# A two-layer hybrid encoder in fp32: all sums of Strassen-like units by accumulating transfers, and two more units in the second mixer

## The chip, the core and the metric

The kernel runs on one core of a Trainium2 chip. The core has five engines that run beside one another, each with its own in-order queue: TensorE (PE; matmuls, with weight loads shown as PEld), VectorE (DVE), ScalarE (ACT), GpSimd (POOL) and SyncE (SP, which only issues transfers here). Transfers (DMAs) are issued by SP, POOL and ACT and run beside the engines; one that adds to its destination, called an accumulating transfer below, is issued by POOL in this kernel. The metric is the device time of one execution in microseconds (us), as the median of several runs.

## What is computed

Two layers over x of 256 positions by 2048 channels, in fp32. Layer 0 mixes with grouped-query attention, layer 1 with dilated windowed attention in three groups of eight heads; each is followed by a gated MLP of width 5632 with a width-3 convolution between its two projections.

```python
def mixer_b(h, w_qkv, w_o, rel_bias):
    qkv = (h @ w_qkv).reshape(b, s, n_g, 3, hg, HEAD_DIM)
    for g, (window, dil) in enumerate(B_GROUPS):
        o, lz = dilated_group(qkv[:, :, g, 0], qkv[:, :, g, 1], qkv[:, :, g, 2], ...)
    ...
    return y @ w_o

def conv_ffn(h, w_up, conv_w, conv_b, w_down):
    u = conv(h @ w_up) + conv_b
    gate, val = jnp.split(u, 2, axis=-1)
    return (jax.nn.silu(gate) * val) @ w_down

for i in range(DEPTH):
    hn = rms_norm(h, mix_norm[i])
    h = h + (mixer_a(hn, ...) if i % 2 == 0 else mixer_b(hn, ...))
    h = h + conv_ffn(rms_norm(h, ffn_norm[i]), ...)
return rms_norm(h, final_norm)
```

## The kernel before

**Matmuls.** All weights stream from DRAM once. A piece of 128 x 1024 fp32 numbers (512 KB) is loaded by SP into a `raw` buffer (a ring of four), and split into a high half `wh` on ACT and a low half `wl` = raw - wh on DVE (rings of four each). Each fp32 product is then three matmuls: high by high, high by low, low by high. `feed` (L142) does this for one group of 512 input channels (`kg`) and 512 output columns: two pieces, 24 matmuls of 128 x 512 in the order in which the pieces come. The splits are given a higher priority, so they stand on ACT and DVE some pieces ahead of their matmuls; how far is limited by the rings.

**Units.** For two column blocks that share their input, one `kg` can be done as a unit: a seven-product scheme on the 2 x 2 blocks b11, b12, b21, b22 of the weights and sums of the inputs. The products, numbered 1, 2, 3, 5, 7, 6, 4 in the order of the code, take 6 matmuls each, 42 in all, where the two plain feeds take 48. Four of the weights that they multiply are sums: t1 = b11 + b12 (product 5), b12 + b22 (product 7), t6 (product 6) and t4 (product 4). `fast_unit` (L190) loads the four blocks and makes the sums with four DVE adds (L204). `home_unit` (L219) makes most of them by transfers: SP loads b11 into t1 and b12 into the second half of a `home` tile, POOL issues accumulating transfers onto b12 (L246) and, after product 1, onto t1 (L248). With two `own` tiles, `middle` (called after the unit's first feed) issues t6 += b12 on POOL (L251) and loads b21 into the other tile by SP (L252), and `rest` does products 2 to 4, with one DVE add (L239) for t4.

**Pairs.** `up_pair` (L636) does a pair of column blocks with a unit for `kg` 0 and plain feeds for `kg` 1 to 3, in an order given by a table: `UP_ORDER` has three feeds of one side, the unit, and three feeds of the other. It then makes the two blocks of the unit's results with folds. The MLP uses it for the gate and value blocks of eight of its eleven pairs of blocks per layer (`UP`), with `home` and `own` tiles; its up and down projections run in two halves (pairs 0 to 5, then 6 to 10), so pair 6 is the first behind the first half's down projection, and its `own` tiles take buffers that the down projection has read. The second mixer (`mixer_b`) runs in two halves (`hf`) of four heads for each of three groups (`g`); `MIX` lists the (hf, g) whose key and query blocks are done as a pair with `fast_unit`, after (0, 0), for which the sums of the inputs are made. (1, 0) makes these sums again and is done plainly, and so are the three value blocks of each half.

**What sets the order.** A scheduler puts each engine's instructions into a fixed order; generators in `pending` and `beside` are advanced one step between feeds, and so place the attention work among the matmuls. On a queue an instruction that waits holds up those behind it. POOL issues the accumulating transfers, and also copies transposed blocks (`tT`, `kT`, `qT`: keys and queries; `wide`: for the values; `u` in the MLP), turns a one-hot table into matmul form in the first MLP (L1368, CAST `oh`, read by PE at L1377), and adds down-projection partial sums to a DRAM copy of the residual (`away`, L325). The residual `h` is kept in the buffers `h0` and `h1`, which are put away in DRAM during some stages (`put_away`, `fetch`) and serve as homes then.

Of the kernel before, what the change touches and what calls it, by code (L numbers as in the profile page):

```python
# [14 lines left out]
P = 128  # L15
# [11 lines left out]
MIX = (0, 1), (0, 2), (1, 1), (1, 2)  # L27
# [9 lines left out]
def tile_encoder(ctx: ExitStack, tc: tile.TileContext, x, xT, w_a, w_ao, q_gain, k_gain, w_b, w_bo,  # L37
# [104 lines left out]
    def feed(accs, lhs, kg, wap, first, last, by_m=False, pieces=1, mid=None, begun=()):  # L142
        raws, w = [], 2048 // pieces
# [10 lines left out]
        def mms(order):  # L154
            for m, kt in order:
                (wh, wl), j = hls[kt // 2], kt % 2
                xh, xl = lhs[4 * kg + kt][:2]
                st, sp = first and kt == 0 and m not in begun, last and kt == 3
# [60 lines left out]
    def home_unit(acc, pick, wap0, wap1, begun, home, end=(1,), own=None):  # L219
# [24 lines left out]
        if own:  # L244
            nc.sync.dma_start(flat(own[0]), wap0[:, :1024])
# [4 lines left out]
        def middle():  # L250
            nc.gpsimd.dma_start(flat(own[0]), flat(b12), accum_op=ALU.add)  # L251
            nc.sync.dma_start(flat(own[1]), wap0[:, 1024:])  # L252

        def rest(end, steps=False):
            if own:
                (t6, b21), b22 = own, raw_tile()
            else:
                b21, b22 = raw_tile(), raw_tile()
                t6 = b22
                nc.sync.dma_start(flat(b21), wap0[:, 1024:])  # L260
            nc.sync.dma_start(flat(b22), wap1[:, 1024:])
            for i, (q, r) in enumerate(((2, b21), (3, b22), (5, t1), (7, b12), (6, t6), (4, b21))):
# [3 lines left out]
                elif q == 7:  # L266
                    total(b21, t6, b21)
# [3 lines left out]
        return (middle, rest) if own else rest  # L271
# [351 lines left out]
    def sums_made(lhs, kg, at, st, picks):  # L623
        own = [pair_slot(at + 2 * i, [P, 4, 2, P], F32R, "s") for i in range(2)]
# [11 lines left out]
    def up_pair(w, ns, lhs, order, picks, junk, fold_tile, first_done, home=None, own=None):  # L636
# [5 lines left out]
        sides = (a2, a4), (a3, a8)  # L642
        tt = nc.vector.tensor_tensor
        for i, (kg, side) in enumerate(order):
            later = {s for _, s in order[i + 1:]}
            if side is None:
# [3 lines left out]
                if home is not None:  # L650
                    rest(end)
                else:
                    fast_unit(acc, picks[kg], w[ns[0], kg], w[ns[1], kg], begun, end, None)
            else:
                mine = ((2, 4), (3, 8))[side]
                feed(sides[side], lhs, kg, w[ns[side], kg], not begun.issuperset(mine),
                     not later & {side, None}, begun=[m for m in range(2) if mine[m] in begun])
                begun.update(mine)
                if i == 0 and home is not None:
                    middle()  # L660
# [18 lines left out]
    def ffn(l, hT, ss_in, cw, g_next, last, side=None):  # L679
        with tc.tile_pool(name=nm("fpool"), bufs=1) as fp:  # L680
# [181 lines left out]
            for hf, (p0, p1) in enumerate(HALVES):  # L862
# [41 lines left out]
                def post(n):  # L904
# [8 lines left out]
                    elif hf == 1:  # L913
                        sumsq_cols(ss, n, junk)
                        start(late_transpose(hTn, n, g_next, fp, "cg", lambda: quad_tile(fp, "quad", 2)))

# [465 lines left out]
    def mixer_b(hT, ss_in):  # L1382
        with tc.tile_pool(name="bpool", bufs=1) as bp:
# [36 lines left out]

            cw, turn = load_taps(1)
            allp = slice(None)
            for hf in range(2):
# [167 lines left out]
                for g in range(3):  # L1591
                    bts = biases(hf, g)
                    ns = 6 * g + 2 + hf, 6 * g + hf
                    if (hf, g) in MIX:
# [8 lines left out]
                        extra[0] = ((hpool, ["a0", "a1"]), (hpool, ["a6", "a7"]), (bp, ["e0", "e1"]))[hf * g]  # L1603
                        qa = up_pair(w_b, ns, hT, MIX_ORDER if (hf, g) == (1, 1) else UP_ORDER, picks, junk, fold_tile, k_done)
                        extra[0] = None
# [118 lines left out]
```

## Time and profile before

| | |
|---|---|
| median of 3 runs | 2214.55 us (2213.77 to 2215.14) |
| profiled execution | 2213.77 us, of which the span is 2211.9 us |
| granted PE clock, mean | 0.999 of full speed |
| DVE, split wl<-raw,wh (L172) | 621 of 1236 ns |
| ACT, split wh<-raw (L171) | 621 of 1044 ns |

The span is the time from the first to the last instruction in the profile. Times in the prediction are those of the profiled execution, counted from the span's start. In the rows, a line such as `L252 SPq DMA_DIRECT2D own<-in_w_up_dram` names the source line, the engine (with q: its queue), the operation and output<-input by the program's names without buffer numbers; "us to landing" is the time from a transfer's issue until its data has arrived. A bracket at a row's end is the time for which the engine was idle before it, and what it then waited for.

### The profile page before, as it was taken

Reading aid. Unit: us, or ns where it says so; the run is one execution under the profiler, and the core shown is the slowest. Engines: PE = TensorE matmul, PEld = TensorE weight load, DVE = VectorE, ACT = ScalarE, POOL = GpSimd, SP = SyncE. Lnnn points to the kernel's source line nnn. Section 1 sums busy time; section 2 is a strip of 40 time slices with the busy share of each in tenths; the row PEclk is TensorE's granted clock in tenths of the full one; section 3 lists DMA queues with packets and bytes.
Section 4 is the critical chain, followed back from the end, with each engine's and each line's share of the span. In section 5 each row is a group of like instructions: output and inputs, shape, how many; then the busy total and the mean of one; then the engine's idle time right before and its main releaser. Section 6 shows DMA issues by size and latency. Waiting matters only on the chain.

```text
span 2211.9 us, 29227 instructions
## 1 busy us (share of the span) xinstructions
PE 2197.0 (99%) x9885; PEld 1821.6 (82%) x9885; DVE 1852.0 (84%) x2335; ACT 1549.9 (70%) x2360; POOL 634.9 (29%) x873
## 2 busy tenths in 40 slices
PE   9999999999999999999999999999999999999998
PEld 7888888888888888888888888888888888888877
DVE  6887779999778998978876878588899987799987
ACT  7667768787457887677756775567878865678764
POOL 3343324432103331041354216003333300223311
PEclk9999999999999999999999999999999999999999
DMA  8666868867988856665566555578777778977754
GB/s 303 194 214 214 274 211 256 246 201 220 284 249 267 238 197 220 209 200 195 184 202 198 173 181 186 193 237 260 229 253 223 224 228 256 299 206 246 232 193 143
DMA packets 141030, 494.13 MB, mean 223 GB/s; under 512 B 15944, under 2 KB 19784, under 8 KB 139856
## 3 DMA queue, kind: packets, MB, share of 16 engines
q1 hardware_dynamic: 125360, 437.44, 58.5%
q0 software_dynamic: 15232, 54.54, 12.0%
q8 instruction: 77, 1.26, 0.2%
q14 instruction: 73, 0.60, 0.1%
q10 hardware_dynamic: 288, 0.30, 0.0%
HBM read 470.09 MB, written 13.73 MB: 219 GB/s over the span
## 4 chain that ended last, share of the span: by engine, by line
PE 55%; DVE 3%; issue 1%; ACT 1%; DMA 0%; POOL 0%; POOLq 0%; DVEq 0%; ACTq 0%
PE acc L161 15%; PE acc L162 15%; PE acc L160 15%; DVE wl L172 1%; PE ps L234 1%; PE ps L233 1%; PE ps L232 1%; PE ps L213 1%; PE ps L212 1%; PE ps L214 1%; PE acc L234 1%; PE acc L233 1%; PE acc L232 1%; PE acc L213 1%; PE acc L214 1%
## 5 line engine op out<-in xcount | busy, mean ns | idle before, releaser
L172 DVE TENSOR_TENSOR wl<-raw,wh 128x1024 fp32r<-128x1024 f32 (+1 forms) x621 | 760.7, 1236 | 163.8 <-ACT wh L171 158.9
L171 ACT ACTIVATE wh<-raw 128x1024 fp32r<-128x1024 f32 (+1 forms) x621 | 642.1, 1044 | 255.3 <-PE acc L162 178.3
L160 PE MATMUL acc<-wh,xh 128*128 128x512 f32 x1668 | 651.5, 391 | 0.5 <-ACT wh L171 0.5
L161 PE MATMUL acc<-wl,xh 128*128 128x512 f32 x1668 | 651.2, 390 | 0.8 <-DVE wl L172 0.7
L162 PE MATMUL acc<-wh,xh 128*128 128x512 f32 x1668 | 650.0, 390 | 0.0
L161 PEld LDWEIGHTS acc<-wl,xh 128*128 128x128 f32 x1668 | 313.5, 188 | 67.3 <-DVE wl L172 3.9
L160 PEld LDWEIGHTS acc<-wh,xh 128*128 128x128 f32 x1668 | 313.6, 188 | 64.7 <-ACT wh L171 1.0
L162 PEld LDWEIGHTS acc<-wh,xh 128*128 128x128 f32 x1668 | 313.3, 188 | 64.5
L751 POOL COPY u<-quad 32x256 f32<-32x256 f32 x352 | 261.9, 744 | 237.5 <-DVE quad L491 219.4
L161 PE MATMUL acc<-wl,a 128*128 128x512 f32 x720 | 280.7, 390 | 1.1 <-DVE wl L172 1.1
L160 PE MATMUL acc<-wh,a 128*128 128x512 f32 x720 | 281.2, 391 | 0.0
L162 PE MATMUL acc<-wh,a 128*128 128x512 f32 x720 | 280.4, 390 | 0.0
L751 ACT ACTIVATE u<-quad 32x256 f32<-32x256 f32 x352 | 147.8, 420 | 20.5 <-DVE quad L491 15.7
L161 PEld LDWEIGHTS acc<-wl,a 128*128 128x128 f32 x720 | 135.3, 188 | 28.9 <-DVE wl L172 1.5
L162 PEld LDWEIGHTS acc<-wh,a 128*128 128x128 f32 x720 | 135.2, 188 | 28.3 <-DVE a L442 0.2
L160 PEld LDWEIGHTS acc<-wh,a 128*128 128x128 f32 x720 | 135.3, 188 | 27.4
L510 POOL COPY wide<-quad 32x256 f32<-32x256 f32 x88 | 53.2, 605 | 210.1 <-DVE quad L491 152.9
L226 ACT ACTIVATE wh<-home 128x1024 fp32r<-128x1024 f32 x65 | 68.2, 1056 | 51.6 <-PE acc L162 45.1
L495 POOL COPY wide<-quad 32x256 f32<-32x256 f32 x133 | 90.6, 681 | 41.6 <-DVE quad L491 31.5
L603 ACT ACTIVATE stg<-acc,rstd 128x512 f32<-128x512 f32 x122 | 80.1, 678 | 31.5 <-DVE acc L675 15.8
L227 DVE TENSOR_TENSOR wl<-home,wh 128x1024 fp32r<-128x1024 f32 x65 | 80.7, 1246 | 16.3 <-ACT wh L226 16.3
L739 DVE SCALAR_TENSOR_TENSOR cg<-u,cw,cg 128x256 f32<-128x256 f32 x176 | 81.7, 509 | 4.5 <-ACT cg L731 4.4
(418 smaller groups left out, 3446.5 us busy)
## 6 DMA issues: line engine op xcount, KB each, us to landing
raw<-in_w_up_dram SPq DMA_DIRECT2D x304, 512.0 KB, 5.2
raw<-in_w_down_dram SPq DMA_DIRECT2D x160, 512.0 KB, 5.4
raw<-in_w_b_dram SPq DMA_DIRECT2D x144, 512.0 KB, 4.7
raw<-in_w_bo_dram SPq DMA_DIRECT2D x48, 512.0 KB, 4.5
raw<-in_w_a_dram SPq DMA_DIRECT2D x40, 512.0 KB, 4.7
raw<-in_w_ao_dram SPq DMA_DIRECT2D x32, 512.0 KB, 4.8
own<-in_w_up_dram SPq DMA_DIRECT2D x32, 512.0 KB, 6.6
home<-in_w_up_dram SPq DMA_DIRECT2D x32, 512.0 KB, 5.1
```

Source lines behind the costliest of these rows:

```text
L160: nc.tensor.matmul(accs[m], xh, wh[:, j, :], start=st, stop=False)
L161: nc.tensor.matmul(accs[m], xh, wl[:, j, :], start=False, stop=False)
L162: nc.tensor.matmul(accs[m], xl, wh[:, j, :], start=False, stop=sp)
L171: nc.scalar.activation(wh[:, c], r[:, c], AF.Copy)
L172: newest[0] = nc.vector.tensor_tensor(wl[:, c], r[:, c], wh[:, c].bitcast(F32), ALU.subtract)
L226: nc.scalar.activation(wh, r, AF.Copy)
L227: newest[0] = nc.vector.tensor_tensor(wl, r, wh.bitcast(F32), ALU.subtract)
L495: nc.gpsimd.tensor_copy(o[32 * c:32 * c + 32, :, 32 * q:32 * q + 32], quad[32 * q:32 * q + 32, c])
L510: nc.gpsimd.tensor_copy(dst, src)
L603: evac[0] = nc.scalar.activation(o[:, m, :], accs[m], AF.Copy, scale=rstd[:, m:m + 1])
L739: nc.vector.scalar_tensor_tensor(cj, halves(flat[:, j, o:o + NT])[:, ::-1], tap(n, j, i), cj, ALU.mult, ALU.add)
L751: put(u[32 * c:32 * c + 32, :, :, 32 * q:32 * q + 32], quad[32 * q:32 * q + 32, c].rearrange("p (j m) t -> p j m t", m=2))
```

## The change

Four things are done.

1. In `home_unit` with `own` tiles, b21 is loaded into t4's tile at the unit's start; product 2 moves from the rest to right behind the first feed; t6 += b12 is issued there, and t4 += t6 is a POOL transfer issued after the next feed. The DVE add of t4 goes.
2. The second mixer's pairs use `home_unit` with `home` tiles in `h0` and `own` tiles in buffers that are free at that time, in place of `fast_unit` and its four DVE adds.
3. There are two more units in the second mixer: the keys and queries of (1, 0), done by `MIX_ORDER`, and the values of groups 0 and 1 of the first half, blocks 4 and 10.
4. For that, the residual goes to DRAM at the end of the first MLP and is fetched in the second half's value part. The sums of the inputs are made once, into `h1`, for both halves.

`feed`'s `last` becomes a list of blocks for which the accumulation ends.

```diff
@@ -24,7 +24,7 @@
 NRAW, NHL = 4, 4
 AHEAD = 60
 UP = 1, 2, 3, 4, 6, 7, 8, 9
-MIX = (0, 1), (0, 2), (1, 1), (1, 2)
+MIX = (0, 1), (0, 2), (1, 0), (1, 1), (1, 2)
 MIX_ORDER = (1, 0), (2, 0), (3, 0), (1, 1), (2, 1), (0, None), (3, 1)
 EVEN = range(0, 16, 2)
 UP_ORDER = (1, 0), (2, 0), (3, 0), (0, None), (1, 1), (2, 1), (3, 1)
@@ -140,6 +140,7 @@
         return x[m] if isinstance(x, tuple) else x[:, m * P:(m + 1) * P]
 
     def feed(accs, lhs, kg, wap, first, last, by_m=False, pieces=1, mid=None, begun=()):
+        last = last if isinstance(last, list) else [0, 1] if last else []
         raws, w = [], 2048 // pieces
         for i in range(max(pieces, 2)):
             if pieces < 4 or i % 2 == 0:
@@ -155,7 +156,7 @@
             for m, kt in order:
                 (wh, wl), j = hls[kt // 2], kt % 2
                 xh, xl = lhs[4 * kg + kt][:2]
-                st, sp = first and kt == 0 and m not in begun, last and kt == 3
+                st, sp = first and kt == 0 and m not in begun, m in last and kt == 3
                 xh, xl = of_m(xh, m), of_m(xl, m)
                 nc.tensor.matmul(accs[m], xh, wh[:, j, :], start=st, stop=False)
                 nc.tensor.matmul(accs[m], xh, wl[:, j, :], start=False, stop=False)
@@ -242,33 +243,41 @@
         nc.sync.dma_start(flat(t1), wap0[:, :1024])
         nc.sync.dma_start(flat(b12), wap1[:, :1024])
         if own:
-            nc.sync.dma_start(flat(own[0]), wap0[:, :1024])
+            t6, t4 = own
+            nc.sync.dma_start(flat(t6), wap0[:, :1024])
+            nc.sync.dma_start(flat(t4), wap0[:, 1024:])
         nc.gpsimd.dma_start(flat(b12), wap1[:, 1024:], accum_op=ALU.add)
         product(1, t1, end)
         nc.gpsimd.dma_start(flat(t1), wap1[:, :1024], accum_op=ALU.add)
 
-        def middle():
-            nc.gpsimd.dma_start(flat(own[0]), flat(b12), accum_op=ALU.add)
-            nc.sync.dma_start(flat(own[1]), wap0[:, 1024:])
+        def plain_steps():
+            product(2, t4)
+            nc.gpsimd.dma_start(flat(t6), flat(b12), accum_op=ALU.add)
+            yield
+            nc.gpsimd.dma_start(flat(t4), flat(t6), accum_op=ALU.add)
+            yield
+            yield
 
         def rest(end, steps=False):
             if own:
-                (t6, b21), b22 = own, raw_tile()
+                b21, b22, s6 = t4, raw_tile(), t6
+                seq = (3, b22), (5, t1), (7, b12), (6, s6), (4, b21)
             else:
                 b21, b22 = raw_tile(), raw_tile()
-                t6 = b22
+                s6 = b22
+                seq = (2, b21), (3, b22), (5, t1), (7, b12), (6, s6), (4, b21)
                 nc.sync.dma_start(flat(b21), wap0[:, 1024:])
             nc.sync.dma_start(flat(b22), wap1[:, 1024:])
-            for i, (q, r) in enumerate(((2, b21), (3, b22), (5, t1), (7, b12), (6, t6), (4, b21))):
+            for i, (q, r) in enumerate(seq):
                 product(q, r, end)
                 if q == 3 and not own:
                     total(b22, t1, b22)
-                elif q == 7:
-                    total(b21, t6, b21)
+                elif q == 7 and not own:
+                    total(b21, s6, b21)
                 if steps:
                     step(i % 2 == 0)
 
-        return (middle, rest) if own else rest
+        return (plain_steps(), rest) if own else rest
 
     def fold(acc, n0, n1, one, two):
         def hs(m, n):
@@ -621,7 +630,11 @@
         yield
 
     def sums_made(lhs, kg, at, st, picks):
-        own = [pair_slot(at + 2 * i, [P, 4, 2, P], F32R, "s") for i in range(2)]
+        if at is None:
+            t = hpool.tile([P, 2, 4, 2, P], F32R, tag="h1", name=nm("s"))
+            own = [t[:, i] for i in range(2)]
+        else:
+            own = [pair_slot(at + 2 * i, [P, 4, 2, P], F32R, "s") for i in range(2)]
         split_in_order(*own, st.rearrange("p i (j t) -> p i j t", j=2))
         pick = {q: tuple(tuple(lhs[4 * kg + b + j][i][:, m * P:(m + 1) * P] for j in range(2)) for i in range(2))
                 for q, b, m in ((1, 0, 0), (2, 2, 0), (4, 2, 1))}
@@ -633,13 +646,15 @@
         yield from sums_begun(lhs, kg, r, st)
         sums_made(lhs, kg, at, st, picks)
 
-    def up_pair(w, ns, lhs, order, picks, junk, fold_tile, first_done, home=None, own=None):
+    def up_pair(w, ns, lhs, order, picks, junk, fold_tile, first_done, home=None, own=None,
+                steps=False):
         (a2, a4), (a3, a8) = new_acc(), new_acc()
         acc, begun = {2: a2, 3: a3, 4: a4, 8: a8}, set()
         if home is not None:
             acc[1] = ps_tile()
             middle, rest = home_unit(acc, picks[0], w[ns[0], 0], w[ns[1], 0], begun, home, own=own)
         sides = (a2, a4), (a3, a8)
+        ended = [] if home is None else [2]
         tt = nc.vector.tensor_tensor
         for i, (kg, side) in enumerate(order):
             later = {s for _, s in order[i + 1:]}
@@ -648,16 +663,17 @@
                 end = [q for q, s in ((1, None), (5, None), (6, None), (7, None), (2, 0), (4, 0), (3, 1))
                        if not later & {None, s}]
                 if home is not None:
-                    rest(end)
+                    rest(end, steps)
                 else:
                     fast_unit(acc, picks[kg], w[ns[0], kg], w[ns[1], kg], begun, end, None)
             else:
                 mine = ((2, 4), (3, 8))[side]
                 feed(sides[side], lhs, kg, w[ns[side], kg], not begun.issuperset(mine),
-                     not later & {side, None}, begun=[m for m in range(2) if mine[m] in begun])
+                     [m for m in range(2) if not later & {side, *([None] if mine[m] not in ended else [])}],
+                     begun=[m for m in range(2) if mine[m] in begun])
                 begun.update(mine)
-                if i == 0 and home is not None:
-                    middle()
+                if home is not None and None in later:
+                    next(middle, None)
             if 0 in begun or not begun >= {1, 2} or later & {0, None}:
                 continue
             begun.add(0)
@@ -913,6 +929,8 @@
                     elif hf == 1:
                         sumsq_cols(ss, n, junk)
                         start(late_transpose(hTn, n, g_next, fp, "cg", lambda: quad_tile(fp, "quad", 2)))
+                        if n % 2:
+                            put_away(n // 2)
 
                 def done(accs, n):
                     add_residual(accs, n)
@@ -1417,6 +1435,10 @@
 
             def fold_tile():
                 return bp.tile([P, 2, 512], F32, tag="vh", name=nm("fold"))
+
+            def homes(pool, *tags):
+                return (hpool.tile([P, 4, 512], F32, tag="h0", name=nm("home")),
+                        [pool.tile([P, 2, 512], F32, tag=t, name=nm("own")) for t in tags])
 
             cw, turn = load_taps(1)
             allp = slice(None)
@@ -1600,25 +1622,35 @@
                             next(gen)
                             beside.append(gen)
 
-                        extra[0] = ((hpool, ["a0", "a1"]), (hpool, ["a6", "a7"]), (bp, ["e0", "e1"]))[hf * g]
-                        qa = up_pair(w_b, ns, hT, MIX_ORDER if (hf, g) == (1, 1) else UP_ORDER, picks, junk, fold_tile, k_done)
-                        extra[0] = None
+                        qa = up_pair(w_b, ns, hT, MIX_ORDER if hf and g < 2 else UP_ORDER, picks, junk, fold_tile, k_done,
+                                     *homes(*((hpool, "a0", "a1"), (hpool, "a2", "a3"), (hpool, "a6", "a7"),
+                                              (bp, "e0", "e1"))[hf * (g + 1)]))
                         start(s_gen(g, qa, kTs[0], bts))
                         continue
                     ka = project(w_b, ns[0], hT, kgs)
                     kT = pair_tile(bp, [P, 4, NT], "kT", 1, g > 0)
                     start(k_gen(ka, kT))
-                    if g == 0:
-                        beside.append(sums(hT, 0, 20, tmp(), tmp(), picks))
+                    beside.append(sums(hT, 0, None, tmp(), tmp(), picks))
                     start(s_gen(g, project(w_b, ns[1], hT, kgs), kT, bts))
                 if hf == 0:
                     start(turn)
-                v12 = [bp.tile([P, 2, 512], F32, tag=f"e{n}", name=nm("v12")) for n in range(2)]
-                for g in range(3):
-                    accs = project(w_b, 6 * g + 4 + hf, hT, kgs)
-                    vs[g] = evac_split(bp, accs, rstd, v12[g - 1] if g else None)
-                    if g == 0:
-                        start(value_stage())
+                def v_whole(g):
+                    return bp.tile([P, 2, 512], F32, tag=f"e{g - 1}", name=nm("v12"))
+
+                def v_done(accs):
+                    vs[0] = evac_split(bp, accs, rstd, None)
+                    start(value_stage())
+
+                if hf == 0:
+                    accs = up_pair(w_b, (4, 10), hT, MIX_ORDER, picks, junk, partial(v_whole, 2), v_done,
+                                   *homes(hpool, "a0", "a1"), True)
+                    vs[1] = evac_split(bp, accs, rstd, v_whole(1))
+                else:
+                    for i in range(2):
+                        fetch(i)
+                    v_done(project(w_b, 5, hT, kgs))
+                    vs[1] = evac_split(bp, project(w_b, 11, hT, kgs), rstd, v_whole(1))
+                vs[2] = evac_split(bp, project(w_b, 16 + hf, hT, kgs), rstd, v_whole(2))
 
             def own(kg):
                 return pair_tile(bp, [P, 4, NT], "qT" if kg else "kT")
```

`order` rows below list an engine's instructions as they stand in its queue: source line, operation, output<-input with buffer numbers, shape, and how many alike follow one another.

ACT, at the first pair of the second half of the first MLP (pair 6). `home_6003` is the unit's home, `own_6005` the tile of b21 and t4, `raw_...` are pieces of the feeds, `ps_6010` is the first product's accumulator. Before:

```order
L226 ACTIVATE wh_6015<-home_6003 128x1024
L171 ACTIVATE wh_6030<-raw_6026 128x1024
L171 ACTIVATE wh_6046<-raw_6028 128x1024
L171 ACTIVATE wh_6068<-raw_6064 128x1024
L171 ACTIVATE wh_6084<-raw_6066 128x1024
L666 ACTIVATE junk_6202<-ps_6010 128x512
L171 ACTIVATE wh_6104<-raw_6100 128x1024
L171 ACTIVATE wh_6120<-raw_6102 128x1024
L226 ACTIVATE wh_6141<-own_6005 128x1024
L226 ACTIVATE wh_6151<-raw_6139 128x1024
L226 ACTIVATE wh_6161<-home_6003 128x1024
```

After:

```order
L227 ACTIVATE wh_6016<-home_6003 128x1024
L172 ACTIVATE wh_6031<-raw_6027 128x1024
L172 ACTIVATE wh_6047<-raw_6029 128x1024
L682 ACTIVATE junk_6202<-ps_6010 128x512
L227 ACTIVATE wh_6063<-own_6005 128x1024
L172 ACTIVATE wh_6078<-raw_6074 128x1024
L172 ACTIVATE wh_6094<-raw_6076 128x1024
L172 ACTIVATE wh_6115<-raw_6111 128x1024
L172 ACTIVATE wh_6131<-raw_6113 128x1024
L227 ACTIVATE wh_6152<-raw_6150 128x1024
L227 ACTIVATE wh_6162<-home_6003 128x1024
```

The first split of `own_6005` stands behind the first feed's two pieces now, where it stood behind three feeds' six; the second and third feeds' splits stand behind it.

POOL, in the first MLP's third pair (pair 3): `home_3799` is its home, `own_3800` its t6, `own_3801` its t4, `oc_3690` the loaded one-hot table and `oh_3691` its matmul form. Before:

```order
L1363 DMA oc_3690<-in_onehot_dram 128x1024
L246 DMA home_3799<-in_w_up_dram 128x1024
L1368 CAST oh_3691<-oc_3690 128x1024
L251 DMA own_3800<-home_3799 128x1024
L751 COPY u_2642<-quad_3640 32x8x32 x8
L248 DMA home_3799<-in_w_up_dram 128x1024
```

After:

```order
L249 DMA home_3799<-in_w_up_dram 128x1024
L1381 DMA oc_3690<-in_onehot_dram 128x1024
L255 DMA own_3800<-home_3799 128x1024
L1386 CAST oh_3691<-oc_3690 128x1024
L767 COPY u_2642<-quad_3640 32x8x32 x8
L251 DMA home_3799<-in_w_up_dram 128x1024
L257 DMA own_3801<-own_3800 128x1024
```

The table's load and its CAST have each gone behind one of the unit's transfers: the CAST stands behind t6 += b12 (L255 after, L251 before), and t4 += t6 (L257) is new.

POOL, in the second half of the second mixer, where the first group's keys (`tT`, first of the two) and queries (second) are copied into place; `bt` are bias tables, `scr` is their place in DRAM. Before:

```order
L1405 DMA bt_2021_10753<-scr 128x2x128 x4
L1405 DMA bt_2022_10754<-scr 128x2x128 x4
L510 COPY tT_10980<-quad_10981 32x8x32 x8
L510 COPY tT_11166<-quad_11167 32x8x32 x8
L510 COPY kT_11491<-quad_11511 32x8x32 x8
```

After, with `home_11177`, `own_11178` and `own_11179` the home, t6 and t4 of the next pair, (1, 1):

```order
L1423 DMA bt_2022_10690<-scr 128x2x128 x4
L249 DMA home_11177<-in_w_b_dram 128x1024
L255 DMA own_11178<-home_11177 128x1024
L251 DMA home_11177<-in_w_b_dram 128x1024
L1423 DMA bt_2023_10691<-scr 128x2x128 x4
L519 COPY tT_11121<-quad_11122 32x8x32 x8
L257 DMA own_11179<-own_11178 128x1024
L519 COPY tT_11225<-quad_11226 32x8x32 x8
```

Three of the next pair's transfers and four bias loads stand ahead of the key copies, and t4 += t6 between the key and the query copies. L255 waits for the landing of L249, and L249 for that of SP's load into the same home.

## The prediction

> **What bounds the kernel now.** I read the page first: the busy shares and the chain that ended last, then what TensorE (PE) waits for.
>
> ```profile
> span 2211.9 us, 29227 instructions
> PE 2197.0 (99%) x9885; PEld 1821.6 (82%) x9885; DVE 1852.0 (84%) x2335; ACT 1549.9 (70%) x2360; POOL 634.9 (29%) x873
> ...
> PE 55%; DVE 3%; issue 1%; ACT 1%; DMA 0%; POOL 0%; POOLq 0%; DVEq 0%; ACTq 0%
> ...
> PE acc L161 <- DVE wl L172: 3.3, 6, 1.1
> ...
> PE ps L457 <- DVE qTl L442: 1.3, 2, 0.8
> ```
>
> PE is occupied for 99% of the span, and its largest waits come to a few us: 3.3 us in six waits for a weight's low half, 1.3 us in two waits for the low half of the queries. VectorE (DVE) is busy 84%, but since PE hardly waits for it, time taken off DVE alone is worth almost nothing. The time is the number of matmuls times their pace, and whatever makes PE wait is added in full, since PE has no slack in which to catch up. The pace stands in the timeline of PE, here where the second half of the first MLP begins:
>
> ```profile
> 640.32 0.39 PE L232 MATMUL ps<-wh,xh 128*128 128x512 f32 x1
> 640.55 0.39 PE L233 MATMUL ps<-wl,xh 128*128 128x512 f32 x1
> 640.78 0.39 PE L234 MATMUL ps<-wh,xh 128*128 128x512 f32 x1
> ...
> 647.12 0.39 PE L160 MATMUL acc<-wh,xh 128*128 128x512 f32 x1
> ```
>
> The listed 0.39 us is a pipelined length; from start to start it is 30 matmuls in 6.80 us, 0.227 us each.
>
> **What the change takes away.** Each unit does with 42 matmuls what two plain feeds do with 48. Two units more are 12 matmuls fewer: 12 x 0.227 = **-2.7 us**. On DVE 32 adds go:
>
> ```profile
> L239 DVE TENSOR_TENSOR own<-own,own x16: 1211/1224/1307, 312.9 to 2023.7; 128x1024 f32<-128x1024 f32 x16
> L204 DVE TENSOR_TENSOR raw<-raw,raw x22: 1210/1220/1305, 895.9 to 2152.4; 128x1024 f32<-128x1024 f32 x22
> ```
>
> All 16 of L239 and 16 of the L204 adds (those of the four mixer units) go, 32 x 1.22 = 39 us of DVE. On PE that is worth no more than the waits above: 3.3 + 1.3 = 4.6 us in all, most at places that the change does not touch. I take **-0.5 us** (0 to -2.5). The new issues on POOL and SP and six more splits on DVE go beside PE work, except where an in-order queue holds something that PE wants soon. These places are the rest of the sum.
>
> **First pair of the second half of each MLP (the largest term).** b21 is now wanted as product 2 right after the first feed. Its buffer is the one that the down projection's last feed has just read, so SP issues the load only when PE is done with that feed, in both kernels at the same place in SP's order. What it took, first MLP and second:
>
> ```profile
> L252 SPq DMA_DIRECT2D own<-in_w_up_dram x1: 328/328/328, 640.5 to 640.5; - x1
> ...
> DMA to landing us min/median/max: 9.0/9.0/9.0
> ...
> L252 SPq DMA_DIRECT2D own<-in_w_up_dram x1: 327/327/327, 1884.0 to 1884.0; - x1
> ...
> DMA to landing us min/median/max: 8.9/8.9/8.9
> ```
>
> Issued at 640.5, landed at 649.5. ACT and PE used it long after that:
>
> ```profile
> 650.04 1.06 ACT L226 ACTIVATE wh<-own 128x1024 fp32r<-128x1024 f32 x1 [1.66 <-PE acc L162]
> ...
> 658.00 0.39 PE L232 MATMUL acc<-wh,xh 128*128 128x512 f32 x1
> ```
>
> Now product 2 stands after 6 matmuls of product 1 and 24 of the first feed, so at 640.32 + 30 x 0.227 = 647.1. Landing 649.5, wh on ACT 1.06 more, 650.6; wl on DVE 1.22 more, 651.8. PE waits 3.5 us for wh, and its second matmul, which wants wl and is due at 647.4, waits about 1.0 us longer: **4.4 us**. In ACT's order the splits of the following feeds stand behind this one, so nothing is done ahead meanwhile. The same numbers hold at 1884.0. Two layers: **+8.8 us**. With the 6.6 us that is the median of all such loads, it would be 647.1 + 2.3 - 647.4 = 2.0 us each; the two rows of this place are nearer, and I keep 2.0 to 4.9 each.
>
> The Trainium skill ("DMA: Bandwidth & Descriptors", section "Anatomy of one DMA — SWDGE (gpsimd) path") gives a fit of 2.0 us plus the bytes over 436 GB/s; as an estimate by that page 512 KB would land 3.2 us after issue, and neither place would stall at all. The trace disagrees: 9.0 and 8.9 us here. The fit is for one DMA by itself; the sum does not use it.
>
> **The sum for product 4, same two places.** t4 += t6 is a transfer on POOL's queue, behind t6 += b12 and two accumulations of down-projection partial sums:
>
> ```profile
> L251 POOL DMA_DIRECT2D own<-home x1: 861/861/861, 647.5 to 647.5; - x1
> ...
> DMA to landing us min/median/max: 8.8/8.8/8.8
> ...
> L325 POOL DMA_DIRECT2D away<-fold x2: 1441/1702/1963, 648.0 to 648.6; - x2
> ...
> DMA to landing us min/median/max: 12.9/14.5/16.0
> ...
> 664.80 0.39 PE L232 MATMUL acc<-wh,xh 128*128 128x512 f32 x1
> ```
>
> t6 has landed at 647.5 + 8.8 = 656.3; only then is t4 += issued. It lands at 664.4 with the 8.0 of the group, or at about 669 with the 12.9 of its neighbours. Product 4 was due at 664.8, now 4.4 later, at 669.2, and needs the data 2.3 before, at 666.9. That is from -2.5 to +2.5; nearer to its own group's row, so **+0.6 us** each, **+1.2** together (0 to 2.5 each).
>
> **One-hot CAST in the first MLP (third pair).** On POOL the CAST now stands behind t6 += b12, which waits for the landing of b12's accumulation:
>
> ```profile
> 370.33 0.87 POOL L246 DMA_DIRECT2D home<-in_w_up_dram  x1 [2.81 <-DMA home<-in_w_up_dram]
> 373.33 1.15 POOL L1368 CAST oh<-oc 128x1024 fp32r<-128x1024 f32 x1 [2.12 <-DMA oc<-in_onehot_dram]
> 379.24 0.87 POOL L251 DMA_DIRECT2D own<-home  x1 [4.76 <-DMA home<-in_w_up_dram]
> ...
> 380.03 0.40 PE L1377 MATMUL ps<-oh,rh 128*24 128x512 f32 x1
> ```
>
> It moves from 373.3 to 379.24 + 0.87 = 380.1 and ends at 381.3; PE reads oh in its order at 380.03: **+1.2 us** (0 to 1.5). The CAST also frees the buffer of this pair's t4, whose load then lands at 381.3 + 6.6 = 388, some 4 us ahead of its use.
>
> **Second mixer, second half, scores of the first group.** Before, POOL's key and query copies had nothing ahead of them. Now the next pair's b12 accumulation, t6 +=, t1 +=, four bias loads and t4 += stand among them.
>
> ```profile
> 1190.51 5.33 POOL L510 COPY tT<-quad 32x256 f32<-32x256 f32 x8 [6.30 <-DVE quad L491]
> 1212.26 5.34 POOL L510 COPY tT<-quad 32x256 f32<-32x256 f32 x8 [16.41 <-DVE quad L491]
> ...
> 1217.64 1.06 ACT L441 ACTIVATE qTh<-tT 128x1024 fp32r<-128x1024 f32 x1 [0.71 <-POOL tT L510]
> ...
> 1218.73 1.23 DVE L442 TENSOR_TENSOR qTl<-tT,qTh 128x1024 fp32r<-128x1024 f32 x1 [2.26 <-ACT qTh L441]
> ...
> 1224.40 0.28 PE L457 MATMUL ps<-kTh,qTl 128*128 128x256 f32 x1
> ...
> raw<-in_w_b_dram SPq DMA_DIRECT2D x144, 512.0 KB, 4.7
> ...
> home<-in_w_up_dram SPq DMA_DIRECT2D x32, 512.0 KB, 5.1
> home<-in_w_up_dram POOLq DMA_DIRECT2D x32, 512.0 KB, 8.6
> own<-home POOLq DMA_DIRECT2D x16, 512.0 KB, 8.0
> ```
>
> Before, qTl was done at 1219.96, 4.4 us ahead of its matmul. By counting matmuls, the home of the pair before is free once its product 7 is split, about 1194.4. Then: load 5.1, 1199.5; accumulation 8.6, 1208.1; issues of t6 += and t1 += 0.87 each and four bias loads, 3.4 at the same price, 1213.2; key copies 5.3, 1218.5; t4 += 0.9 and query copies 5.3, 1224.7; qTh 1.06 and qTl 1.23, 1227.0 against 1224.4. That is 2.6; I take **+2.4 us**, since the bias loads may be a little cheaper. The accumulation is not shown with these weights: with a raw load's 4.7 for it, the chain loses 3.9 and nothing stalls; with 12.9 it is 6.9 us.
>
> **Smaller places.** The value copies of the second mixer stand behind such a landing too; in the trace
>
> ```profile
> 1153.18 21.60 POOL L495 COPY wide<-quad 32x256 f32<-32x256 f32 x32 [2.90 <-DVE quad L491]
> 1176.11 0.60 PE L1553 MATMUL ps<-wide,v 128*128 128x128 f32 x4
> ```
>
> the copies end 1.3 us ahead of the matmul, and 0.9 us of each new issue comes off that; with the first copies of that mixer **+0.6 us** (0 to 4). The other units I counted through: their sums land 2 us or more ahead, cost nothing, and the residual's trip to DRAM and back (away<-h, h<-away) has a whole projection as cover. Without that cover it is a stall of one landing, some 6 to 7 us.
>
> **Sum.** -2.7 - 0.5 + 8.8 + 1.2 + 1.2 + 2.4 + 0.6 = **+11.0 us**. The profiled execution took 2213.8 us (span 2211.9 and 1.9 around it), 0.8 below the median of the runs, 2214.55, and inside what separates them (2213.77 to 2215.14). So 2213.8 + 11.0 = **2224.8 us**.
>
> **Rivals.** (a) *Transfers land in time, and the matmuls are what is left*: 2213.8 - 2.7 - 0.5, to -2.5, is 2208.6 to 2210.6. The mechanism is b21's landing at 640.5 and 1884.0; it decides at 4.5 us after issue (647.4 - 2.3 - 640.5). For it: raw loads have a median of 4.7. Against it: both rows of this place show twice 4.5, the load moves nowhere in SP's order, and the same neighbours are in flight. This is the side where the change is faster. (b) *Only the MLP's two places stall, and mildly*: with 2.0 to 4.4 each, the CAST, and neither the scores nor t4 += late, 2213.8 - 3.2 + 4.0 to 8.8 + 1.2 = 2215.8 to 2220.6. (c) *POOL's queue is worse than counted*: t4 += at 2.5 each (+3.8 over my value), scores at 6.9 (+4.5), the small places at 4 (+3.4): up to 2236.5; half of that is 2230.6. For it: the 12.9 us landing beside the MLP. (d) *The change doesn't do what it says*: with the same number of matmuls the first term is lost, 2227.5; the new order has 12 fewer, so hardly.
>
> **Chances and range.** My forecast, 2220.6 to 2229, has 0.55; (b) 0.22, of which 0.07 lies below 2219 and 0.04 of that below 2217; (c) 0.17, of which 0.09 lies above 2231; (a) 0.05; (d) 0.01. A difference under 0.2% (4.4 us, so 2210.1 to 2219.0 is no change) is what a measurement of this kernel can hardly tell. Faster: the lower part of (a), 0.03. Same: the rest of (a) and the 0.07 of (b), 0.09. Slower: 0.88. The range leaves out (a), the lower edge of (b) and the upper half of (c), 0.05 + 0.04 + 0.09 = 0.18: 2217 to 2231.
>
> **What would show it.** In the new trace: PE with 12 fewer matmuls; at 647 and 1890 a wait of PE for wh and wl of own, 3.5 and 1.0 us; at 669 a short wait for the split of product 4; at 380 a wait of L1377's successor for the CAST on POOL; before the scores at 1224 a wait for qTl, with POOL's key copies standing behind a landing. Wrong would be: b21 landing within 4.5 us of its issue; its split not the one that PE waits for; or waits of more than 2 us at pairs that I count as free, which would mean that the accumulations in the mixer land much later than in the MLP.

## The result and the profile after

The changed kernel took 2240.4 us (median of 4 runs, 2238.08 to 2243.79) against 2214.6 before (4 runs): ratio 1.0116, 95% interval [1.0101, 1.0131]. It is slower, as forecast, but by 26 us where the forecast of 2224.8 us lay 10 above before, and it lies 9 us above the range. The profiled execution took 2242.32 us, its span 2240.5, 28.6 more than before's 2211.9.

The busy row of after's page, and its list of what PE waited for (us in all, times, longest; three rows under 1 us are left out):

```profile
PE 2205.9 (98%) x9873; PEld 1823.8 (81%) x9873; DVE 1823.8 (81%) x2316; ACT 1554.9 (69%) x2367; POOL 654.5 (29%) x917
```

```profile
PE acc L162 <- DVE wl L173: 7.4, 10, 1.7
PE acc L233 <- ACT wh L227: 6.3, 2, 3.7
PE ps L464 <- DVE a L451: 2.6, 1, 2.6
PE ps L464 <- ACT qTh L450: 2.5, 1, 2.5
PE ps L466 <- DVE qTl L451: 2.1, 3, 0.8
PE ps L572 <- DVE warm L569: 1.5, 1, 1.5
PE ps L1395 <- POOL oh L1386: 1.3, 1, 1.3
PE acc L234 <- DVE wl L228: 1.1, 2, 0.6
```

PE has 12 instructions fewer (9885 to 9873), and DVE 28 us less to do. The waits for wh and wl of an own tile (L227, L228), for qTh, qTl and oh are the forecast ones. Two of the larger rows are not: the first, ten waits for plain pieces' low halves (before had six, 3.3 us), and the third, in the value stage. All listed waits add up to 26.7 us against 7.3 before, 19 more; with the 2.7 us of matmuls taken off, 12 us of the 28.6 are still missing. About 2 of them are restarts: a wait is listed from the end of a matmul's 0.39 us, but without it the next one would start 0.227 us behind the last, so each of the twelve waits more costs 0.16 us beyond its listed length. The rest is in the pace. The timeline of PE at pair 6 of the second MLP:

```profile
1913.18 0.39 PE L163 MATMUL acc<-wh,xh 128*128 128x512 f32 x1
1916.23 0.64 PE L233 MATMUL acc<-wh,xh 128*128 128x512 f32 x1 [2.67 <-ACT wh L227]
1917.49 0.79 PE L234 MATMUL acc<-wl,xh 128*128 128x512 f32 x1 [0.62 <-DVE wl L228]
1918.09 0.63 PE L235 MATMUL acc<-wh,xh 128*128 128x512 f32 x1
1918.51 0.63 PE L233 MATMUL acc<-wh,xh 128*128 128x512 f32 x1
...
1922.78 0.62 PE L162 MATMUL acc<-wl,xh 128*128 128x512 f32 x1
1923.20 0.43 PE L163 MATMUL acc<-wh,xh 128*128 128x512 f32 x1
1923.47 0.39 PE L161 MATMUL acc<-wh,xh 128*128 128x512 f32 x1
```

Behind the wait the matmuls follow one another every 0.427 us instead of 0.227, until 1923. The stretches of after say why (length, then PE, PEld, DVE, ACT and POOL busy, then the granted clock, DMA share, GB/s):

```profile
647.00:652.00 5.00, 1.35 (x5) 0.69 (x4) 0.47 (x1) 1.55 (x2) 3.10 (x3) 0.81 0.92 279
652.00:657.00 5.00, 4.53 (x11) 3.31 (x11) 4.72 (x5) 3.40 (x4) 0.88 (x1) 0.51 1.07 167
657.00:664.00 7.00, 7.00 (x33) 5.75 (x32) 3.12 (x3) 2.12 (x2) 0.00 (x0) 1.00 1.07 265
...
1916.00:1923.00 7.00, 6.15 (x14) 4.53 (x15) 5.86 (x5) 4.08 (x5) 0.88 (x1) 0.53 1.11 237
```

The granted clock falls to half behind a long wait. Counted from the start-to-start times, the slow matmuls cost 2.0 us at 647, 1.9 at 1199, 3.1 at 1247 and 2.8 at 1916: some 9.8 us that are no wait in any list.

### The profile page after: what moved, and what is told of

It reads as the page before. It is cut to its first block, busy times and chain, and to the rows that moved or that the text cites. A ratio compares the mean times of both kernels' runs of the same rounds, so it can differ in the third digit from the quotient of the medians.

```text
span 2240.5 us, 29342 instructions
## 1 busy us (share of the span) xinstructions
PE 2205.9 (98%) x9873; PEld 1823.8 (81%) x9873; DVE 1823.8 (81%) x2316; ACT 1554.9 (69%) x2367; POOL 654.5 (29%) x917
## 4 chain that ended last, share of the span: by engine, by line
PE 50%; DVE 4%; DMA 3%; ACT 1%; issue 1%; POOL 1%; POOLq 0%; DVEq 0%; SPq 0%; ACTq 0%
PE acc L162 14%; PE acc L163 14%; PE acc L161 14%; DMA raw<-in_w_b_dram 2%; DVE wl L173 1%; PE ps L233 1%; PE ps L234 1%; PE ps L235 1%; PE acc L234 1%; PE acc L235 1%; PE acc L233 1%; ACT wh L172 1%; DMA away<-h 0%; POOL tT L519 0%; DMA home<-in_w_b_dram 0%
## 5 line engine op out<-in xcount | busy, mean ns | idle before, releaser
L173 DVE TENSOR_TENSOR wl<-raw,wh 128x1024 fp32r<-128x1024 f32 (+1 forms) x612 | 748.6, 1233 | 171.8 <-ACT wh L172 166.6
L172 ACT ACTIVATE wh<-raw 128x1024 fp32r<-128x1024 f32 (+1 forms) x612 | 633.8, 1045 | 263.3 <-PE acc L163 150.2
L162 PE MATMUL acc<-wl,xh 128*128 128x512 f32 x1632 | 639.5, 392 | 5.7 <-DVE wl L173 5.6
L161 PE MATMUL acc<-wh,xh 128*128 128x512 f32 x1632 | 639.3, 392 | 0.9 <-ACT wh L172 0.9
L163 PE MATMUL acc<-wh,xh 128*128 128x512 f32 x1632 | 637.6, 391 | 0.0
L161 PEld LDWEIGHTS acc<-wh,xh 128*128 128x128 f32 x1632 | 308.2, 189 | 65.0 <-ACT wh L172 1.5
L163 PEld LDWEIGHTS acc<-wh,xh 128*128 128x128 f32 x1632 | 307.8, 189 | 64.0
L767 POOL COPY u<-quad 32x256 f32<-32x256 f32 x352 | 248.8, 707 | 219.4 <-DVE quad L500 201.4
L228 DVE TENSOR_TENSOR wl<-home,wh 128x1024 fp32r<-128x1024 f32 x83 | 103.2, 1249 | 28.7 <-ACT wh L227 28.7
L227 ACT ACTIVATE wh<-home 128x1024 fp32r<-128x1024 f32 x83 | 87.3, 1055 | 50.5 <-PE acc L163 46.3
L228 DVE TENSOR_TENSOR wl<-own,wh 128x1024 fp32r<-128x1024 f32 x57 | 69.7, 1226 | 38.6 <-ACT wh L227 38.2
L227 ACT ACTIVATE wh<-own 128x1024 fp32r<-128x1024 f32 x57 | 60.2, 1056 | 56.0 <-PE acc L163 30.4
```

What stands on the lines that cost most here:

```text
L161: nc.tensor.matmul(accs[m], xh, wh[:, j, :], start=st, stop=False)
L162: nc.tensor.matmul(accs[m], xh, wl[:, j, :], start=False, stop=False)
L163: nc.tensor.matmul(accs[m], xl, wh[:, j, :], start=False, stop=sp)
L172: nc.scalar.activation(wh[:, c], r[:, c], AF.Copy)
L173: newest[0] = nc.vector.tensor_tensor(wl[:, c], r[:, c], wh[:, c].bitcast(F32), ALU.subtract)
L227: nc.scalar.activation(wh, r, AF.Copy)
```

## Experiments

Each ratio is against the kernel before, run on the same chip; kernels of one group shared a chip, and groups are compared by ratios.

**Which part loses.** `mlp_only` is before with the MLP's part of the change alone. `mixer_only` is after with

```diff
+            if late:
+                nc.gpsimd.dma_start(flat(t6), flat(b12), accum_op=ALU.add)
+                nc.sync.dma_start(flat(t4), wap0[:, 1024:])
...
```

in all of the MLP's units, and product 2 back in the rest, with the DVE add. (Its mixer units are those of after; that they use the old scheme too, as its expectation says, does not hold for the kernel that ran.)

> The kernel before with the MLP's part of the change alone (home_unit and up_pair of after; the second mixer as before, so no fewer matmuls). If the two places at pair 6 cost what the trace of after shows there (waits of 4.8 and 3.9 us and the halved clock's 2.0 and 2.8), plus the CAST's 1.5 and 1.1 at 690 us, then about 2213.8 + 16 - 1 = 2229 us (2225 to 2232), with PE waits for wh<-own of about 3.6 us twice. Rival, that the second mixer carries the whole loss: 2217 us or less.

> After, with the MLP's units as they were before (b21 loaded behind the first feed, product 2 in the rest, t4 by a DVE add; the same scheme in the mixer's units too, which keep their accumulations for b12, t1 and t6). If the loss is the sum of both parts: 2240 - 16 = 2224 us (2220 to 2229), the waits at pair 6 gone, the waits for late raw pieces in the mixer (971 to 1195 us) still there. If the mixer carries it all: 2237 or more.

2229.1 us, ratio 1.0059 [1.0044, 1.0074], and 2230.0 us, 1.0060 [1.0043, 1.0076]: each part carries half. `mlp_only` shows the two waits for wh<-own, 7.4 us together, and hardly any of the mixer's. `mixer_only` came out 1 us above its expected range.

**The buffer of b21.** `p6_slot` is after with one condition changed, so that pair 6's own tiles lie in buffers that the down projection has read some feeds earlier:

```diff
-[pair_slot(kt + (20 if p < p0 + 2 or hf == 0 else 12), ...
+[pair_slot(kt + (20 if p == p0 + 1 or hf == 0 else 12), ...
```

> After, with pair 6's two own tiles in buffers that the down projection has read some feeds earlier (those of kg 3), so that b21's load waits for no late reader. If the buffer makes the load late: both waits for wh<-own go, and with them the halved clock behind them, 6.8 + 6.6 = 13.4 us, 2227 us (2224 to 2230). Rival, that transfers beside one another make it late wherever it is issued: under 4 us gained, 2237.

2226.0 us, ratio 1.0056 [1.0038, 1.0074]: 14 us gained by the medians, 13 by the ratios, and its trace shows no wait for own at pair 6 in either layer. b21 is loaded from 609.2 us on there, where after loads it from 641.1 on, and lands in 7.1 us, still more than the 4.5 that the prediction's rival (a) asked for. So the late buffer made b21 late; the slow landing alone does no harm.

**Is it idleness that halves the clock?** `p6_busy` is after with, at pair 6 of both layers,

```diff
+            if busy is not None:
+                acc[5] = ps_tile()
+                for _ in range(15):
+                    nc.tensor.matmul(acc[5], busy[0][:, :P], busy[2], start=True, stop=True)
             product(2, t4)
```

> After, with 15 matmuls without use put between the first feed and product 2 at pair 6 of both layers, so that PE is busy (15 x 0.227 = 3.4 us) while it would wait for b21; their result is overwritten. If idleness of PE halves its clock: the granted clock stays 1.0 behind product 2, and 2.0 + 2.8 us are gained, 2235.5 us, though the data come no earlier. Rival, that the clock falls for another reason, or that the slow matmuls are only late data: the paces of 0.427 us stay, and the time is 2240 or more.

2236.7 us, ratio 1.0094 [1.0079, 1.0109], near the 2235.5 expected: by the medians 4 us gained by matmuls that do nothing, though the interval just overlaps after's. The trace is plainer. Its timeline of PE, and then its stretches, at the same place:

```profile
651.68 3.56 PE L257 MATMUL ps<-xh 128*128 128x512 f32 x15
655.28 0.50 PE L233 MATMUL acc<-wh,xh 128*128 128x512 f32 x1
656.54 0.50 PE L234 MATMUL acc<-wl,xh 128*128 128x512 f32 x1 [0.76 <-DVE wl L228]
656.88 0.40 PE L235 MATMUL acc<-wh,xh 128*128 128x512 f32 x1
657.11 0.40 PE L233 MATMUL acc<-wh,xh 128*128 128x512 f32 x1
```

```profile
647.00:652.00 5.00, 5.00 (x24) 4.14 (x23) 1.69 (x2) 0.04 (x1) 0.00 (x0) 1.00 1.01 315
652.00:657.00 5.00, 4.21 (x18) 2.96 (x17) 1.74 (x2) 2.83 (x3) 3.10 (x3) 1.00 0.95 211
```

Product 2 still comes 3.6 us late, but the clock stays 1.00 and the pace 0.23 us. A wait of PE costs its length, and a long one the halved clock on top.

**Why plain pieces are late in the mixer.** The transfers of raw pieces from 1060 to 1260 us, by line, of before and then of after, with who waited for them (us, times):

```profile
L150 SPq DMA_DIRECT2D raw<-in_w_b_dram x62: 327/328/487, 1069.3 to 1250.5; - x62
...
  ACT wh L171: 4.5, 2
...
DMA to landing us min/median/max: 3.6/4.5/6.4
```

```profile
L151 SPq DMA_DIRECT2D raw<-in_w_b_dram x53: 327/328/820, 1059.8 to 1257.8; - x53
...
  ACT wh L172: 24.9, 11
...
DMA to landing us min/median/max: 3.4/5.4/10.9
```

The longest landings stand beside accumulating transfers: three pieces issued from 1181 to 1187 took 9.4 to 10.9 us while t1 += (1179.8) and t4 += (1186.9) were under way. ACT, in order, waits for them, and at 1195 an evacuation behind such a split held up PE for 2.6 us. Four kernels, all with p6_slot's buffers, ask what it is:

```text
 mix_dve_sums:  - up_pair(..., *homes(...))   + up_pair(...) with extra raw buffers, so fast_unit, four DVE adds
 mix_plain_dma: - accum_op=ALU.add            + accum_op=ALU.bypass   (the mixer's units only)
 mix_ring2:     + extra[0] = two more raw buffers in three of the key/query pairs
 mix_ring:      the same and the value pair
```

> p6_slot (2226 us) with all six mixer units' sums by DVE adds again (fast_unit, four adds each, with extra raw buffers as before the change); the two units more and the residual's way over DRAM are kept. If the accumulating transfers are the mixer's loss, as traffic that slows the raw loads and as POOL issues ahead of the score copies: the 17 us of waits and halved clock that p6_slot's trace shows from 1000 to 1250 us nearly all go, about 2211 us (2209 to 2215). Rival, that the two more units or the residual's transfers are the loss: 2222 or more.

> p6_slot with the mixer's accumulating transfers made plain copies on the same queue, of the same size (so the sums of its units are left out and the mixer's result is not the reference's). If it is the adding in the transfers that takes the DMA engines' time: raw loads beside them land in about 5 us instead of 8 to 12, and 5 us or more are gained, 2221 or less. If it is the bytes and the issues alone: under 2 us, 2224 or more.

> p6_slot (2226 us) with two more raw buffers for the first half's two key/query pairs and for the pair (1, 1) alone (mix_ring's third place, the value pair, ran into a 14.7 us wait for a buffer that the probabilities still held, so it told nothing). If the shallower ring is why PE waits for raw pieces: the waits at 1002, 1047 and 1090 us (0.7 + 0.6 + 2.0) go, about 2223. If the slow landing beside accumulating transfers is: at least half of them stay, 2225 or more. In both, raw pieces still land in 8 us and more beside those transfers.

> p6_slot (2226 us) with two more raw buffers beside the ring of four again, as the mixer's pairs had them before the change, here in buffers that are free during the first half's two key/query pairs, the value pair and the pair (1, 1); the pair (1, 0) has none. If the raw pieces come late because the change took these buffers: the waits for wl<-raw between 1000 and 1150 us and the one at 1192 (with its halved clock) go, 6 to 9 us, 2217 to 2220. If the loads are slow beside the accumulating transfers, and more buffers don't help: under 2 us, 2224 or more. The waits before the scores (1237 to 1250) stay in both.

`mix_dve_sums`: 2220.4 us, 1.0021 [1.0012, 1.0031], better than p6_slot by 6 us by the medians and 8 by the ratios, where 15 were expected: it lies between the two answers that its expectation names. In its trace the stall in the value stage (p6_slot: 2.2 us) is gone, with a wait of 1.5 us for POOL's copies of the values in its place, and ACT's waits for raw pieces from 1000 to 1260 us come to 7.0 us, where p6_slot has 33.8. But this kernel has the spare raw buffers too, its pieces still land in a median of 5.2 us and 8.2 at most, and PE's waits for plain pieces' low halves still come to 5.8 us (p6_slot: 7.7). So the accumulating transfers are a part of the mixer's loss, and not all of it. `mix_plain_dma`, which leaves out the mixer's sums: 2225.2 us, 1.0035 [1.0024, 1.0047], by its time on the side of bytes and issues. Yet its transfers onto home land sooner, and so do its raw pieces (from 1000 to 1260 us a median of 4.9 us and 8.6 at most, where p6_slot has 5.4 and 10.4), and its stall in the value stage is 0.3 us. The median landings of the former, p6_slot's, then its own:

```profile
home<-in_w_b_dram POOLq DMA_DIRECT2D x12, 512.0 KB, 9.0
```

```profile
home<-in_w_b_dram POOLq DMA_DIRECT2D x12, 512.0 KB, 6.9
```

So a transfer that adds lands later than one that copies, and loads beside it do too; but the interval overlaps p6_slot's, and what that is worth in time is not settled. `mix_ring2`: 2227.4 us, 1.0049 [1.0034, 1.0064], where 2223 was expected if the ring was the cause. Pieces still land in up to 10.5 us; in its trace the waits at 1047 and 1090 us are gone and the one at 1000 is 0.5, so spare buffers do cover slow landings there, but no gain shows in the times. `mix_ring` (2241.3 us, 1.0113 [1.0098, 1.0128], expected 2217 to 2220) ran into a 14.4 us wait of its own making, so it does not bear on the question.

**What the two more units are worth alone.** `two_more_units` is mix_dve_sums with the MLP as before; the next two undo one unit each; `mlp_slot` is mlp_only with p6_slot's line.

> mix_dve_sums with the MLP's units as before the change, too, so that the two units more are all that is left of the change: 12 matmuls fewer, 2.7 us. Expected 2212 us (2209 to 2216), faster than before by 0.1%. Rival, that a unit costs in waits what it saves in matmuls: 2215 or more.

> two_more_units (2220 us) without the unit of (1, 0), whose keys and queries are done plainly as before the change (6 matmuls more, 1.4 us). If the pair makes the scores wait, since its keys and queries leave the folds late and close together: the wait before the scores at 1230 us (2.9 and 1.6 with the halved clock) goes, 2217 us (2215 to 2219). Rival, that something later or the residual's transfers make that wait: it stays, and the time is 2221 or more.

> two_more_units (2220 us) without the value pair, whose blocks are done plainly (6 matmuls more, 1.4 us). If the value pair makes PE wait for its raw pieces at 1140 us (2.1 and 1.7) and for the wide copies at 1189 (1.7): they go, 2216.5 us (2214.5 to 2219), and the wait before the scores stays. Rival: these waits stay, 2221 or more.

> mlp_only (2229 us) with pair 6's own tiles in the early buffers. If the late buffer is the MLP part's whole loss but for the CAST (1.4 us): 2229.1 - 7.4 - 7.9 = 2214 to 2217 us, the same as before the change, so that 16 DVE adds fewer (20 us of DVE) are worth nothing that shows. Rival, that adds off DVE are worth time once the stall is gone: 2211 or less.

In this order: 2220.1 us, 1.0020 [1.0010, 1.0029]; 2216.2, 0.9997 [0.9988, 1.0007]; 2215.9, 1.0000 [0.9990, 1.0009]; 2216.7, 1.0001 [0.9992, 1.0010]. The first missed its range of 2209 to 2216, and the other three lie in theirs. Each part, mended, is worth nothing that can be measured: a unit saves 1.4 us of matmuls and makes about 2 us of waits (2.0 for a plain piece at 1142 in value_pair_only, 2.2 for qTh at 1225 in keyquery_pair_only), and 16 DVE adds fewer leave the time where it was. The two units together are slower than either: at 1230 the wait is 2.7 us. By the ratios, the 26 us of after are some 13 for pair 6's late buffer (p6_slot), 8 for the mixer's accumulating transfers with their fewer raw buffers (mix_dve_sums) and 4 to 5 for the two units together (two_more_units).

**The wait before the scores.** In after POOL's rows are the ones that the prediction counted through:

```profile
1227.79 0.87 POOL L255 DMA_DIRECT2D own<-home  x1 [7.37 <-DMA home<-in_w_b_dram]
1228.36 1.18 POOL L251 DMA_DIRECT2D home<-in_w_b_dram  x1
1228.90 3.58 POOL L1423 DMA_DIRECT2D bt<-scr  x4
1232.52 5.53 POOL L519 COPY tT<-quad 32x256 f32<-32x256 f32 x8
1238.01 0.93 POOL L257 DMA_DIRECT2D own<-own  x1
1240.47 5.28 POOL L519 COPY tT<-quad 32x256 f32<-32x256 f32 x8 [1.53 <-DVE kTl L451]
```

But mix_dve_sums, with none of these transfers, still waits 2.7 us for qTh: a pair's keys and queries leave their folds late and together, while the scores kept their place. Three kernels put the scores one feed later (23 or 24 matmuls, 5.4 us, and not the 2.7 that the first expectation says):

```diff
-for _ in range(0 if g == 0 else 1 + hf * (g == 1)):
+for _ in range(2 * hf if g == 0 else 1 + hf * (g == 1)):
```

> keyquery_pair_only (2215.9 us) with the scores of (1, 0) placed one feed (2.7 us) later in the program. If the pair's scores wait only because its queries leave the folds later than plain ones while the scores kept their place: the wait of 2.3 us before them goes, about 2213.5 us (2212.5 to 2215). If the whole chain of copies simply moves along: the wait stays, 2215.5 or more.

> two_more_units (2220.1 us) with the same shift of the scores. Placement alone: the wait of 2.9 us and the halved clock's 1.6 behind it go, 2215.6 us (2214 to 2217.5). Otherwise 2219 or more.

> p6_slot (2226.0 us), in which the next pair's accumulating transfers stand ahead of the key and query copies on POOL, with the same shift. The wait of 3.8 us falls to about 1.1 and the clock is not halved any more: 6 us, 2220 us (2218 to 2222.5). If the POOL queue has more in hand than this feed covers, or the clock falls anyway: 2223.5 or more.

keyquery_pair_only so changed: 2215.6 us, 0.9999 [0.9990, 1.0007]; two_more_units: 2220.0, 1.0015 [1.0006, 1.0024]; p6_slot: 2222.9, 1.0030 [1.0020, 1.0040]. None reached its expected range. In all three traces the wait before these scores is gone. With p6_slot the 3.8 us of waiting and 3.1 of halved clock are gone with it, and 3 us of time by the medians (the intervals just overlap). In the other two about as much came back at 1273 us, where PE now waits 2.2 and 2.1 us for POOL's copies of the next group's queries: the chain of copies moved along. No kernel here beats the one before clearly.

Single traces must not be compared too finely. All these kernels run the same instructions in the same order on every engine up to 160 us, and yet at 154 us PE waits 2.3 us for pTh in value_pair_only's trace, 1.1 in p6_slot's, and not at all in after's. The trace of p6_slot is also of its longest execution, 2234.5 us against a median of 2226.0. Differences of a few us are therefore read from the medians here, and the traces say where a wait is.

## Why the prediction was wrong

The direction and the forecast places were right, the size was not. Two steps of the prediction failed: it priced a wait of PE at its length alone, and it took the mixer's plain pieces to land as before.

- **Matmuls**, -2.7: 12 fewer, as said.
- **Pair 6**, 4.4 each: PE waited 3.65 us for wh and 0.47 for wl at 647, and 2.67 and 0.62 at 1913, in the trace's lists; with the restarts 4.8 and 3.9. p6_slot shows the cause named, a late buffer. The fit that the prediction set beside this place is one for GpSimd's transfers, as the title of its section says; b21 is loaded by SP, and landed 9.2 and 8.2 us after its issue.
- **"Whatever makes PE wait is added in full"** is the first step that failed. A wait was priced at its length, with 0.227 us for all that follows. Behind these two places 2.0 and 2.8 us more were lost to the halved clock, and some 9.8 us at all four. p6_busy shows that it is PE's idleness that does it. The trace of before had a sign, which was not read: 11 matmuls at the kernel's start, after an idle PE, take 5.06 us, 0.46 each.

```profile
1.45 5.06 PE L563 MATMUL ps<-warm 128*128 128x512 f32 x11 [1.45 <-DVE warm L560]
```

  The Trainium skill ("TensorE: Matmul & The Clock Gate", section "What's actually happening") says that the clock is halved after an idle window of about 3.4 us and comes back after a busy one. The trace agrees in the length of the low stretches (1199.6 to 1203.1 us is 3.4 us, and the other three last 6.8, twice that); in the idle time it differs, since 2.2 us of it between 646.7 and 650.1 were enough.
- **t4 += at pair 6**, 0.6 each: no wait for product 4 in either layer. In the first it was issued at 654.6, 1.7 us sooner than counted, and landed in 10.9 us; PE's 6.8 us of delay ahead of product 4 gave it time.
- **CAST**, 1.2: 1.3 by the list.
- **Scores**, 2.4: 2.5 + 0.8 us of waits and 3.1 of clock. The queue was the right mechanism but not the only one: 2.7 us of wait stay without it.
- **"Smaller places", 0.6 (0 to 4)** is the second step that failed: "their sums land 2 us or more ahead, cost nothing". The sums did land in time. What was not counted is that the plain pieces beside them would come late: the waits for wl from 971 to 1152 us came to about 7 us, and the value stage's stall at 1195, with its clock, to 4.6. Together 11.6. mix_dve_sums and mix_plain_dma show that the accumulating transfers have a part in it; how much is theirs, and how much the missing raw buffers', the residual's transfers' or the two units', stays open. The sign that was named for this, a wait of more than 2 us at a place counted as free, did come, but not for the reason given with it: the accumulations landed in a median of 9.2 us in the mixer, against 8.7 in the MLP.
- **Waits that go**, -0.5: about 3 us went, a little more than the bound of 2.5.

With them the terms make -2.7 + 6.8 + 6.6 + 1.5 + 6.9 + 11.6 + 1.1 (a new wait at 690 us, before pair 7's first product) - 3 = 28.8, against 28.6 in the spans.

## What to carry to other kernels

On a PE that is busy 99%, price a wait in two parts: its length, and, from some 2 us up, one to three more for the clock behind it. Before moving a load earlier in the program, look at who last read its buffer. Making a sum by an accumulating transfer takes nothing off the path if the engine that made it before was not on it, and here it slowed the loads that were.

## What was not expected of the hardware

In the traces of all 17 kernels the granted clock changes only at the steps of a grid of 3.41 us, whose place differs from trace to trace. In after it is low from 650.1 to 656.9, 1199.6 to 1203.1, 1247.4 to 1254.2 and 1916.4 to 1923.3 us: for two, one, two and two steps, beginning whole numbers of steps apart. What decided was how long PE idled within one step. Over all the traces, up to the last matmul, the 28 steps with 1.96 us or more were all followed by one at half the clock, 5 of the 12 with 1.6 to 1.95 were, and hardly any with less. So a wait of 2.0 to 2.3 us halved the clock at some places and not at others, and one of 2.7 us, at 1230 in mix_dve_sums, did not: 1.75 us of it fell into one step and the rest into the next. A low stretch cost 1 to 3 us.

And a 512 KB accumulating transfer from DRAM took 9.0 us where the same copy on the same queue took 6.9.
